# A hybrid attention and delta-rule layer on one core: a price for product changes in the planner, the last transposes in runs of eight, and a new slab order

## The chip, the cores and the metric

The kernel runs on one core of one Trainium2 chip. The metric is the device time of one execution in microseconds (us). Each time is the median of several executions of the same program.

## What is computed

One layer of a bidirectional encoder trunk: 512 tokens, 1024 channels, float32 throughout. In short:

```python
h = rms_norm(x, norm_pre)
aq, ak, av, az, dq, dk, dv, db, da, dz, gate_att, gate_dn = split_cols(h @ w_in)

q, k = rope(rms_norm(heads(aq))), rope(rms_norm(heads(ak)))       # 8 and 2 heads of 128
o_att = softmax(q @ k.T / sqrt(128)) @ v
y_att = (o_att * silu(az)) @ w_br_att

qkv = silu(short_conv(concat(dq, dk, dv), conv_w))                # 5 taps, 8 heads of 128
o_dn = bidir_gated_deltanet(l2(q), l2(k), v, decay(da), beta(db)) # chunks of 64, both directions
y_dn = (rms_norm(o_dn) * silu(dz)) @ w_br_dn

mix = (sigmoid(gate_att) * y_att + sigmoid(gate_dn) * y_dn) @ w_out
x1 = x + rms_norm(mix, norm_post)
out = x1 + rms_norm(sigmoid(x1 @ w_ple_gate) * (p @ w_ple_proj), ple_norm)
```

Inside the delta rule each chunk needs the inverse of a unit triangular matrix, and a scan over the chunks in each direction carries a state per head.

## The kernel before

**Two kinds of products.** The wide projections run as sums of three products of rounded parts: each operand is split into a high part and a low part, and low x high, high x low and high x high are added up. One step is three products with 512 columns; eight steps make one *slab* of 128 output channels (`gemm_t`, L542 to L559). These are called long products here. The delta rule, and the transposes by TensorE, use plain float32 products with 128 columns or fewer. These are the short ones.

**Two chains.** The delta rule is done for two groups of four heads, one after the other. `chain` starts `phase_a` (products of keys with keys and queries, then the substitution and the block steps of the inverse) and then two generators of `phase_b`, one for each direction; these are the scan. In a scan each product (L1202, L1213, L1222, L1240, L1254, four heads at once) waits for an operation of VectorE or ScalarE on the one before it. `phase_y` normalises the result of a group and transposes it.

**The planner.** The order of every instruction on each engine is made in Python when the kernel is built, by the class `Flow`. Parts of the kernel are generators, each with a priority (a smaller number goes first). They yield what they want: a time (`at`), an event (`ev`), a free buffer (`get`), or TensorE for so many us (`pe`). `Flow.run` (L124 to L157) keeps a clock, takes the ready part with the best priority, and moves the clock on by the time of TensorE that the part names, 0.682 us for a step of three long products, 0.9 us for four heads of short ones. Operations of the other engines are given a duration, find the first free place in a list of their engine's busy times (`fit`, `slot`, `op`), and are put into the program in that order of time. On the chip the order on each engine is what this gave; the times are what the hardware makes of them.

**The stream of slabs.** One generator, `stream`, with the last priority 10, goes through the list ORDER: `dq`, `dk`, `dv` (delta queries, keys and values by head), `dz`, `az`, `gA`, `gB` (gates), then the blocks `kv`, `q0`, `q1`, and behind the attention `ydn`, `yatt`, `out0`, `out1`, `pg0`, `pg1`. So TensorE does a step of a slab whenever no short product is ready. The weights are loaded from HBM in the same order (`fetch`, the queue of SyncE), and split in `loader`: the high part by ScalarE, the low part by VectorE or GpSimd (POOL). `split` (L254 to L266) chooses POOL if it ends sooner than VectorE plus a margin, COOL in general, HOT while `chains` is above 0, which is during the substitution and the probability products of the heads.

**Attention heads and what follows.** `att_heads` does four heads: sixteen score products, softmax without its division, then sixteen blocks of probabilities that are split on ScalarE and VectorE and multiplied with the values (L1734) in a ring of buffers in unit u14. Scores take a bank of PSUM of the kind `mm` while more than SPAREMM of them are free, and of the kind `aux` otherwise. The first two slabs of `yatt` are done together (`yatt_two`, L1838 on): their first half needs the first head group, their second half the second group. `vec` in the list starts the loads of the two vectors of the last norms (`vec_load`).

**The end.** `out0` and `out1` make the mix for four blocks of 128 rows. `out1_tail` adds the normalised mix to x, giving x1, and brings x1 into transposed form for the last products: row block 0 through VectorE and the DMA queues, blocks 1 to 3 by TensorE, for each half of 512 channels a scaling, four transposes (L1969) and a split. `pg0` and `pg1` are the gate products of the per-layer input.

**Other numbers.** SPARE lists windows of the planner's clock in which unused buffers are lent to the loader (`lend`). EXPS is a margin by which `prep` chooses between four exponentials on ScalarE (L983) and an addition on VectorE with one exponential (L987). EOUT is the earliest time on the planner's clock at which the product of p is stored; VGAP is the distance of the loads of values. PR holds priorities.

Of the kernel before, what the change touches and what calls it, by code (L numbers as in the profile page):

```python
# [35 lines left out]
class Flow:  # L36
# [7 lines left out]
    def __init__(self, slots):  # L44
        self.now = 0.0
        self.eng = {}
        self.slots = {k: [0.0] * n for k, n in slots.items()}
        self.parts = []
        self.later = []
        self.n = self.steps = 0  # L50
        self.shut, self.link = None, lambda a, b: None

# [66 lines left out]
    def flush(self):  # L119
        while self.later and self.later[0][0] <= self.now + 1e-9:  # L120
            _, _, fn, a, k = heapq.heappop(self.later)
            fn(*a, **k)  # L122

    def run(self):  # L124
        while self.parts:
            best, soon = None, None
            for p in self.parts:
                r = self.ready(p[3])
                if r is None:
                    continue  # L130
                if r <= self.now + 1e-9:
                    if best is None or p[:2] < best[:2]:
                        best = p
                elif soon is None or r < soon:
                    soon = r
            if best is None:
                if soon is None:
# [7 lines left out]
            try:  # L145
# [4 lines left out]
                continue  # L150
            if want[0] == "pe":
                self.now += want[1]
                self.steps += 1
                want = ("at", self.now)
# [5 lines left out]
ORDER = """  # L160
dq1 dk2 dk1 dk0 dq3 dk3 dq0 dq2 dv2 az4 dq6 az3 dk5 dv3 dq4 gB6
gA2 dk4 az7 dz1 dz4 dv1 gB5 dz2 az6 dv0 gB0 dq5 dq7 dk6 gB4 dk7
gA0 az0 gB3 dz6 dv6 dv7 gA6 gA5 dv4 dz0 az2 kv dv5 gB2 vec gA7
gB1 az1 dz3 az5 gA3 dz5 q0 dz7 gA1 q1 gA4 gB7 free_h ydn1 ydn2 ydn6
ydn3 ydn0 ydn5 ydn7 ydn4 yatt7 yatt4 yatt6 heads_on0 yatt3 yatt5 yatt0 yatt2 yatt1 heads_on1 out0
out1 pg0 pg1
"""
OUT0 = 'yatt3 yatt1 yatt2 yatt4'
PR = dict(dec=5, dm1=2, y=7, conv=1, gate=6, kv=4, q=9, head=7, ple=9, prep=1, tab=9)
GAP = 0.0  # L170
EXPS = 0.11
SP13 = 480.0
SPARE = ((15, "raw", 7.0, 190.0), (11, "pair", 22.0, 80.0), (12, "pair", 22.0, 80.0), (14, "pair", 279.0, 375.0),
         (13, "pair", 443.0, SP13), (6, "pair", 560.0, 640.0), (14, "raw", 590.0, 640.0))
EOUT = 27.01
WIDE = 2.0
LAND = "c2"
QTURN = (0,)
TURNED = 1
# [4 lines left out]
PVB = 0.695  # L184
VGAP = 1.5
HEADHOT = 1
BATCH, TURN = 4, 0.3
SPAREMM = 2
W1 = 0
COOL, HOT = 10.41, -0.29  # L190


@with_exitstack
def layer(ctx, tc, x, xT, pw0, wp1, wt, wba, wn, rows, qkn, hd16, npost, pnorm, dnorm, cs, out):
# [42 lines left out]
    def unit(i, shape, dt=F32):  # L237
        return tile(f"u{i}", shape, dt)
# [220 lines left out]
    slab, blocks, fetched = {}, {}, {}  # L459
    taken, weighed = Event(), Event()  # L460

# [3 lines left out]
    def lend(u, kind, t0, t1):  # L465

        yield "at", t0
        yield "get", f"u{u}"
        w = unit(u, [128, 2, 1024], F32 if kind == "raw" else F32R)
# [1162 lines left out]
    def att_heads(g):  # L1632
# [61 lines left out]
        yield "get", "u14"  # L1694
        ring = unit(14, [128, 2, 2, 16, 32], F32R)
        for i in range(2):
            F.slots[f"ring{i}"] = [F.now]
# [238 lines left out]
    def out1_tail(t, o, need):  # L1936
# [10 lines left out]
        for half, src in enumerate((late["mx0"][:, t, :], o)):  # L1947
# [5 lines left out]
            if t < TURNED:  # L1953
# [8 lines left out]
                ends.append((L, te))  # L1962
                continue
            yield "at", tr + 0.3
            yield "get", "aux"
            pt = bank("aux", [128, 4, 128])
            for j in range(4):
                k = half * 4 + j
                pe.transpose(pt[:, j, :], xa[:, k * 128:(k + 1) * 128], ident)  # L1969
            yield "pe", 0.436  # L1970
            cc = slice(t * 128, (t + 1) * 128)
            _, te = split(pt, x1Th[half][:, :, cc], x1Tl[half][:, :, cc], F.now, 512)
            free("aux", te)
        for half, (L, te) in enumerate(ends):
            yield "at", te - 0.5
            te = landed(L, te, x1Th[half], x1Tl[half], t)
        return te + 0.2
# [271 lines left out]
```

## Time and profile before

| | us |
|---|---|
| median of 3 runs | 733.78 |
| the three runs | 733.13, 733.86, 733.78 |
| the profiled execution | 732.72 |
| its span | 731.0 |

The profile holds one execution. PE is TensorE's products, PEld its weight loads, DVE is VectorE, ACT ScalarE, POOL GpSimd, SP SyncE. In rows of the timeline stand start, duration, engine, line, operation, output and input by the program's names, and in brackets the idle time ahead and what ended it. Products are pipelined: a product of 512 columns is shown with 0.39 us, while the next starts 0.23 us later. The kernel's two chains lie between 88 and 427 us, the heads between 490 and 600, the end of the list behind that. Most of VectorE's operations carry the line of a helper (L97 or L122), so they are told apart by their tiles: `whi` and `wlo` are a slab's high and low part, `wraw` what was loaded, `mm` and `aux` banks of PSUM, `u` a large unit of SBUF, `c`, `f`, `blk`, `go`, `gi` smaller buffers.

### The profile page before, as it was taken

The page shows a single profiled execution, that of the slowest core. Times are in us where ns is not written, and L with a number is a line of the kernel's source. Part 1 is how long each engine was busy: PE and PEld are TensorE (multiplying, and loading weights), DVE is VectorE, ACT ScalarE, POOL GpSimd, SP SyncE. Part 2 cuts the span into 40 slices and gives each one's busy share as a digit, 9 for nine tenths or more (in the row PEclk, how much of TensorE's full clock was granted, in tenths as well). Part 3 has the DMA queues.
Part 4 walks back from the last instruction along what each step waited for, and adds up shares of the span by engine and source line. Part 5 has one row for each costly group of instructions (what it writes and reads, how often), then busy time and mean ns, then how long its engine had stood idle before and what let it go on. Part 6 is the DMA issues. An engine that isn't in the chain of part 4 may idle for free.

```text
span 731.0 us, 12273 instructions
## 1 busy us (share of the span) xinstructions
PE 718.7 (98%) x4577; PEld 601.3 (82%) x4577; DVE 496.2 (68%) x914; ACT 352.6 (48%) x669; POOL 307.4 (42%) x293
## 2 busy tenths in 40 slices
PE   9999999999999999999999999999999999999996
PEld 7688888888789898888888888888888778888885
DVE  4688979889785667896946443658979974314534
ACT  6658653753651365435442236345746554323522
POOL 5836495111421265114411145655344638163501
PEclk9999999999999999999999999999999999999999
DMA  9854529856421324767350234695468568337313
GB/s 355 301 175 133 195 87 282 265 173 230 103 96 37 101 101 113 234 202 201 121 158 15 87 115 142 198 226 155 163 196 207 192 220 309 135 95 256 110 57 117
DMA packets 79051, 121.64 MB, mean 166 GB/s; under 512 B 24400, under 2 KB 42768, under 8 KB 78992
## 3 DMA queue, kind: packets, MB, share of 16 engines
q1 hardware_dynamic: 78848, 120.73, 52.4%
q8 instruction: 36, 0.59, 0.3%
q14 instruction: 23, 0.19, 0.1%
q10 hardware_dynamic: 144, 0.13, 0.1%
HBM read 94.98 MB, written 25.85 MB: 165 GB/s over the span
## 4 chain that ended last, share of the span: by engine, by line
PE 85%; DVE 8%; ACT 3%; issue 2%; DMA 1%; POOL 1%; POOLq 0%; SPq 0%; DVEq 0%; ACTq 0%
PE mm L553 15%; PE mm L555 14%; PE mm L554 14%; PE mm L574 4%; PE mm L572 4%; PE mm L573 4%; PE mm L592 3%; PE mm L590 3%; PE mm L591 3%; DVE f L122 3%; PE aux L1222 2%; PE aux L1254 2%; PE aux L1240 2%; PE aux L1213 1%; PE aux L1202 1%
## 5 line engine op out<-in xcount | busy, mean ns | idle before, releaser
L553 PE MATMUL mm<-u,wlo 128*128 128x512 f32 x488 | 195.9, 402 | 0.4 <-DVE wlo L97 0.4
L555 PE MATMUL mm<-u,whi 128*128 128x512 f32 x488 | 190.4, 390 | 0.0
L554 PE MATMUL mm<-u,whi 128*128 128x512 f32 x488 | 190.2, 390 | 0.0
L102 POOL TENSOR_TENSOR wlo<-wraw,whi 128x1024 fp32r<-128x1024 f32 x47 | 113.0, 2406 | 178.4 <-ACT whi L122 146.9
L553 PEld LDWEIGHTS mm<-u,wlo 128*128 128x128 f32 x488 | 91.8, 188 | 19.7 <-ACT u L122 0.8
L555 PEld LDWEIGHTS mm<-u,whi 128*128 128x128 f32 x488 | 91.6, 188 | 19.7
L554 PEld LDWEIGHTS mm<-u,whi 128*128 128x128 f32 x488 | 91.8, 188 | 17.0
L122 ACT CAST whi<-wraw 128x1024 fp32r<-128x1024 f32 x61 | 63.9, 1047 | 57.6 <-PE mm L555 20.1
L122 DVE SCALAR_TENSOR_TENSOR f<-mm,cw,f 128x510 f32<-128x510 f32 (+1 forms) x96 | 71.4, 746 | 9.0 <-ACT f L122 6.6
L102 POOL TENSOR_TENSOR u<-wraw,u 128x1024 fp32r<-128x1024 f32 x18 | 43.1, 2403 | 27.6 <-ACT u L122 26.0
L572 PE MATMUL mm<-u,u 128*128 128x512 f32 (+1 forms) x136 | 51.8, 381 | 0.0
L574 PE MATMUL mm<-u,u 128*128 128x512 f32 (+1 forms) x136 | 51.3, 377 | 0.0
L573 PE MATMUL mm<-u,u 128*128 128x512 f32 (+1 forms) x136 | 51.2, 377 | 0.0
L122 DVE TENSOR_TENSOR u<-aux,u 128x512 f32<-128x512 f32 (+2 forms) x49 | 31.6, 664 | 12.9 <-PE aux L1043 6.4
L122 ACT COPY c<-aux 128x512 f32<-128x512 f32 x18 | 10.4, 585 | 48.2 <-DVE f L122 35.4
L590 PE MATMUL mm<-whi,u 128*128 128x512 f32 x80 | 31.4, 393 | 0.0
L122 ACT ACTIVATE mm<-f 128x512 f32<-128x512 f32 x24 | 14.4, 600 | 35.0 <-DVE f L122 35.0
L592 PE MATMUL mm<-whi,u 128*128 128x512 f32 x80 | 31.2, 390 | 0.0
L591 PE MATMUL mm<-wlo,u 128*128 128x512 f32 x80 | 31.1, 389 | 0.0
L102 POOL TENSOR_TENSOR u<-u,u 128x1024 fp32r<-128x1024 f32 (+1 forms) x11 | 22.0, 2004 | 20.9 <-ACT u L122 15.6
L574 PEld LDWEIGHTS mm<-u,u 128*128 128x128 f32 x136 | 25.6, 188 | 4.8
L573 PEld LDWEIGHTS mm<-u,u 128*128 128x128 f32 x136 | 25.6, 188 | 4.6
(297 smaller groups left out, 1504.2 us busy)
## 6 DMA issues: line engine op xcount, KB each, us to landing
wraw<-in_wt_dram SPq DMA_DIRECT2D x58, 512.0 KB, 3.6
wraw<-in_wn_dram SPq DMA_DIRECT2D x24, 512.0 KB, 4.1
u<-in_wt_dram SPq DMA_DIRECT2D x14, 512.0 KB, 6.3
u<-CI SPq DMA_DIRECT2D x16, 256.0 KB, 5.5
u<-VD SPq DMA_DIRECT2D x16, 256.0 KB, 6.7
u<-in_x_dram SPq DMA_DIRECT2D x4, 512.0 KB, 7.6
u<-in_xT_dram SPq DMA_DIRECT2D x4, 512.0 KB, 8.2
eD<-u SPq DMA_DIRECT2D x8, 256.0 KB, 9.0
```

Source lines behind the costliest of these rows:

```text
L102: ins = fn(*a, **k)
L122: fn(*a, **k)
L553: pe.matmul(o, lo[:, k, :], mh(k), start=(k == 0), stop=False)
L554: pe.matmul(o, hi[:, k, :], ml(k), start=False, stop=False)
L555: pe.matmul(o, hi[:, k, :], mh(k), start=False, stop=(k == 7))
L572: pe.matmul(o, b, hi, start=(i == 0), stop=False)
L573: pe.matmul(o, a, lo, start=False, stop=False)
L574: pe.matmul(o, a, hi, start=False, stop=(i == 7))
L590: pe.matmul(o[t], b, hi, start=(k == 0), stop=False)
L591: pe.matmul(o[t], a, lo, start=False, stop=False)
L592: pe.matmul(o[t], a, hi, start=False, stop=(k == 7))
L1222: pe.matmul(pw[:, h, :], Vm[g][d][:, 4 * c + h, :], r[:, h, :], start=True, stop=True)
```

## The change

Three things are changed.

1. `Flow.run` knows which generators make short products in float32 (`is_exact`). Whenever TensorE goes from one of them to any other part, the planner's clock is moved on by SWAP = 0.09 us. A new method, `later_than`, can hold such a part back for up to DEFER us, if another one will be ready by then, and let the stream go first. DEFER is 0.0.
2. In `out1_tail`, for row blocks 1 to 3, the two halves are scaled first, then eight transposes stand in one run over two banks, then the two splits.
3. ORDER, OUT0 (the places of out0's loads among the slabs), priorities and margins are other ones. In ORDER `vec` moves from the middle to a place behind the last `yatt`. One lending of u14 (from 590 us of the planner's clock) now waits until the second head group has taken its ring there.

```diff
+    def is_exact(p):
+        return p[2].__name__ in ("phase_a", "phase_b", "phase_y", "q_tail", "kv_tail", "out1_tail")
+
+    def later_than(self, p):
+
+        since = self.put.setdefault(p[1], self.now)
+        if self.now >= since + DEFER or not any(
+                q is not p and self.is_exact(q) and q[3][0] == "at" and self.now < q[3][1] <= since + DEFER for q in self.parts):
+            self.put.clear()
+            return None
+        ways = [q for q in self.parts if not self.is_exact(q) and q[2].__name__ == "stream" and q[3][0] == "at"
+                and q[3][1] <= self.now + 1e-9]
+        return ways[0] if ways else None
...
+            if best is not None and not self.exact and self.is_exact(best):
+                best = self.later_than(best) or best
...
             if want[0] == "pe":
+                exact = self.is_exact(best)
+                if self.exact and not exact:
+                    self.now += SWAP
+                self.exact = exact
                 self.now += want[1]
...
-dq1 dk2 dk1 dk0 dq3 dk3 dq0 dq2 dv2 az4 dq6 az3 dk5 dv3 dq4 gB6
-gA2 dk4 az7 dz1 dz4 dv1 gB5 dz2 az6 dv0 gB0 dq5 dq7 dk6 gB4 dk7
-gA0 az0 gB3 dz6 dv6 dv7 gA6 gA5 dv4 dz0 az2 kv dv5 gB2 vec gA7
-gB1 az1 dz3 az5 gA3 dz5 q0 dz7 gA1 q1 gA4 gB7 free_h ydn1 ydn2 ydn6
-ydn3 ydn0 ydn5 ydn7 ydn4 yatt7 yatt4 yatt6 heads_on0 yatt3 yatt5 yatt0 yatt2 yatt1 heads_on1 out0
+dq2 dk3 dk2 dk0 dq3 dk1 dq0 dq1 dv2 az2 dk6 dv3 dq7 dq6 dk5 gA2
+dz5 az0 dv1 dz7 dz4 gB0 az5 dz2 gA3 az3 dv0 gB2 dk7 dq4 dq5 gB1
+dk4 dz1 gA4 az1 dv6 dv4 gB7 gB4 dz0 dv7 kv dv5 az4 gB5 gA1 gA7
+gB6 gB3 gA0 dz3 q0 az7 az6 dz6 q1 gA6 gA5 free_h ydn4 ydn1 ydn5 ydn6
+ydn2 ydn0 ydn3 ydn7 yatt2 heads_on0 yatt0 yatt6 yatt3 yatt5 yatt4 yatt1 yatt7 vec heads_on1 out0
 out1 pg0 pg1
-OUT0 = 'yatt3 yatt1 yatt2 yatt4'
-PR = dict(dec=5, dm1=2, y=7, conv=1, gate=6, kv=4, q=9, head=7, ple=9, prep=1, tab=9)
+OUT0 = 'yatt3 yatt7 yatt6 yatt0'
+PR = dict(dec=1, dm1=2, y=9, conv=1, gate=6, kv=5, q=0, head=5, ple=1, prep=3, tab=3)
-EXPS = 0.11
+EXPS = -0.24
-EOUT = 27.01
+EOUT = 25.2
+SWAP, DEFER = 0.09, 0.0
-VGAP = 1.5
+VGAP = 1.2
-SPAREMM = 2
+SPAREMM = 1
-COOL, HOT = 10.41, -0.29
+COOL, HOT = 9.89, -1.3
...
+        if u == 14 and t0 > 500.0:
+            yield "ev", ringed
...
-            yield "at", tr + 0.3
+        for half, (L, te) in enumerate(ends):
+            yield "at", te - 0.5
+            te = landed(L, te, x1Th[half], x1Tl[half], t)
+        if t < TURNED:
+            return te + 0.2
+        yield "at", tr + 0.3
+        pts = []
+        for half in range(2):
             yield "get", "aux"
-            pt = bank("aux", [128, 4, 128])
+            pts.append(bank("aux", [128, 4, 128]))
+        for half, pt in enumerate(pts):
             for j in range(4):
                 k = half * 4 + j
                 pe.transpose(pt[:, j, :], xa[:, k * 128:(k + 1) * 128], ident)
-            yield "pe", 0.436
+        yield "pe", 0.872
```

More of the change, by code (lines that the diff above doesn't have):

```diff
@@ L50, in __init__ @@
         self.n = self.steps = 0
+        self.exact, self.put = False, {}
         self.shut, self.link = None, lambda a, b: None
@@ L122, in flush @@
             fn(*a, **k)
+    @staticmethod
+    def is_exact(p):
[9 more added lines that the diff above has]
+        return ways[0] if ways else None
     def run(self):
@@ L459, in layer @@
     slab, blocks, fetched = {}, {}, {}
-    taken, weighed = Event(), Event()
+    taken, weighed, ringed = Event(), Event(), Event()
     lent = {"raw": {}, "pair": {}}
@@ L1695, in att_heads @@
         ring = unit(14, [128, 2, 2, 16, 32], F32R)
+        if g == 1:
+            ringed.set(F.now)
         for i in range(2):
@@ L1962, in out1_tail @@
                 ends.append((L, te))
-                continue
-            yield "at", tr + 0.3
+        for half, (L, te) in enumerate(ends):
[6 more added lines that the diff above has]
+        for half in range(2):
             yield "get", "aux"
-            pt = bank("aux", [128, 4, 128])
+            pts.append(bank("aux", [128, 4, 128]))
+        for half, pt in enumerate(pts):
             for j in range(4):
@@ L1969, in out1_tail @@
                 pe.transpose(pt[:, j, :], xa[:, k * 128:(k + 1) * 128], ident)
-            yield "pe", 0.436
-            cc = slice(t * 128, (t + 1) * 128)
+        yield "pe", 0.872
+        cc = slice(t * 128, (t + 1) * 128)
+        for half, pt in enumerate(pts):
             _, te = split(pt, x1Th[half][:, :, cc], x1Tl[half][:, :, cc], F.now, 512)
             free("aux", te)
-        for half, (L, te) in enumerate(ends):
-            yield "at", te - 0.5
-            te = landed(L, te, x1Th[half], x1Tl[half], t)
         return te + 0.2
```

## The prediction

> **What bounds the kernel now.** I read the head of the page first, then the waits of TensorE (PE), then the stages, then PE's rows in order of time.
>
> ```profile
> span 731.0 us, 12273 instructions
> PE 718.7 (98%) x4577; PEld 601.3 (82%) x4577; DVE 496.2 (68%) x914; ACT 352.6 (48%) x669; POOL 307.4 (42%) x293
> PE 85%; DVE 8%; ACT 3%; issue 2%; DMA 1%; POOL 1%; POOLq 0%; SPq 0%; DVEq 0%; ACTq 0%
> ```
>
> PE is busy for 98% of the span, and 85% of the chain that ends last is PE. The change adds and removes no product, so nearly all of the 718.7 us stays. What an order can win is in the other 731.0 - 718.7 = 12.3 us. The waits of PE, longest first, say where some of it lies:
>
> ```profile
> PE mm L2110 <- POOL ident masks.py:199: 1.4, 1, 1.4
> PE mm L1861 <- DVE u L97: 0.7, 1, 0.7
> PE aux L1132 <- issue: 0.7, 1, 0.7
> PE mm L1861 <- POOL wlo L102: 0.6, 1, 0.6
> ...
> PE mm L881 <- DVE partk L122: 0.3, 1, 0.3
> ...
> PE aux L1486 <- DVE f L97: 0.3, 1, 0.3
> ```
>
> The 1.4 us ahead of the warm-up stay. The others shown are 0.7 + 0.7 + 0.6 + 0.3 + 0.3 = 2.6 us. Two of the three longest are in L1861, the first product group of the attention branch's output, which stands around the second head group's probability products.
>
> ```profile
> 90.00:190.00 100.00, 100.00 (x471) 83.62 (x471) 86.70 (x156) 55.52 (x121) 38.92 (x35) 1.00 0.68 204
> 210.00:265.00 55.00, 54.94 (x392) 49.42 (x391) 34.45 (x91) 21.52 (x41) 17.82 (x14) 1.00 0.22 72
> 530.00:600.00 70.00, 68.65 (x581) 55.42 (x582) 58.11 (x88) 40.06 (x73) 32.28 (x33) 1.00 0.63 194
> 600.00:725.00 125.00, 123.93 (x581) 103.41 (x579) 48.98 (x73) 43.52 (x77) 54.83 (x44) 1.00 0.47 164
> 725.00:731.00 6.00, 0.00 (x0) 0.00 (x0) 1.83 (x5) 0.81 (x3) 1.53 (x3) 0.82 0.26 87
> ```
>
> The columns are the stretch, its length, and busy time of PE, PEld, DVE, ACT and POOL, then the granted clock. In the substitution (90 to 190) PE has no gap, with DVE at 86.7%. In the first chain (210 to 265) PE lacks 0.06 us. The head stage (530 to 600) lacks 1.35 us, the largest loss in the middle. Behind 725 PE has ended and the last row is stored. The clock is 1.00 wherever PE works, so nothing is to be had there.
>
> A busy PE hides short waits, since the end of a product is modelled. Adding up start-to-start distances beyond the usual ones, I get waits of some 6 to 7 us behind the start, all told; this is my estimate, and the cap of any gain.
>
> **The price of a change.** The planner now adds 0.09 us to its clock whenever a long product follows a short one. What does such a change cost?
>
> ```profile
> 671.18 0.39 PE L573 MATMUL mm<-u,u 128*128 128x512 f32 x1
> 671.41 0.39 PE L574 MATMUL mm<-u,u 128*128 128x512 f32 x1
> 671.64 0.60 PE L1969 MATMUL aux<-ident,whi 128*128 128x128 f32 x4
> 671.99 0.48 PE L572 MATMUL mm<-u,u 128*128 128x512 f32 x1
> 672.31 0.40 PE L573 MATMUL mm<-u,u 128*128 128x512 f32 x1
> ...
> 238.69 0.39 PE L555 MATMUL mm<-u,whi 128*128 128x512 f32 x1
> 238.92 1.05 PE L1254 MATMUL aux<-c,u 128*128 128x128 f32 x8
> 239.73 0.48 PE L553 MATMUL mm<-u,wlo 128*128 128x512 f32 x1
> 240.05 0.39 PE L554 MATMUL mm<-u,whi 128*128 128x512 f32 x1
> ```
>
> The first long product behind a run (671.99, 239.73) shows 0.48 us for 0.39, and 0.32 to the next start for 0.23: that looks like a price of 0.09. But it also starts early. From the last long product before the run to the second behind it: 672.31 - 671.41 = 0.90 with four short ones, 240.05 - 238.69 = 1.36 with eight. Two long ones take 2 x 0.23 = 0.46 of each. So four short ones and a change take 0.44, eight and a change 0.90; the difference gives 0.115 for a short one, and 0.44 - 0.46 = -0.02 for the change. Within the 0.01 of the rows' rounding, **a change costs 0 to 0.01 us**, not 0.09.
>
> The Trainium skill ("TensorE: Matmul & The Clock Gate", section "LDWEIGHTS (loading the stationary operand)") puts a weight load at its columns over 1.2 GHz, 107 ns for 128. If that load of the first long product stood bare behind a run, three changes fewer at the end would give 3 x 0.107 = 0.32 us (an estimate from that page). The rows above show no such cost, and the sum goes by them.
>
> **The change part by part.**
>
> *Price.* No instruction is added. The code yields at most 62 short groups in each chain (8 of keys and queries, 16 of the inverse, 34 in the two scans, 4 of the transposes behind) and 14 in the tails of kv, q and x1: 138 x 0.09 = 12.4 us at most by which the planner's clock runs slower; it does not set instructions' durations, only their order. In each gap of a scan that is filled with steps of three long products (0.68 us), 0.09 is 13% of a step; so some 13% of the gaps may get one step fewer. 68 scan groups x 0.13 = 9 gaps. Each costs between 0 (the operand was ready) and 0.68 us: 0 to 6 us. I take 0.05 a gap, +0.45 us, because the first chain's 55 us today lack only 0.06, that is, operands are mostly ready when PE comes.
>
> *Holding back.* DEFER is 0.0, so the test in later_than is true on its first call, and it always returns None. Nothing is held. 0 us.
>
> *x1 in runs of eight.* Rows 1 to 3 do both halves' scaling first, then eight transposes, then the splits. Three changes fewer: 0 to 0.03 us. The first half is ready later by one scaling and half a run, about 1.2 us; who waits?
>
> ```profile
> 690.90 0.69 DVE L122 TENSOR_TENSOR u<-aux,u 128x512 fp32r<-128x512 f32 x1 [1.20 <-ACT u L122]
> ...
> 696.48 0.39 PE L573 MATMUL mm<-u,u 128*128 128x512 f32 x1
> ```
>
> The last split of row 3 ends at 691.6; its gate product starts near 696.5. The cover is 4.9 us, and a second bank of aux is free there. 0 us.
>
> *Norm vectors later.* Their two loads are moved behind the last yatt slab.
>
> ```profile
> 595.00 0.64 SPq L122 DMA_DIRECT2D blk<-in_npost_dram  x1
> 596.58 0.33 SPq L122 DMA_DIRECT2D blk<-in_pnorm_dram  x1
> ...
> 639.19 0.69 DVE L122 TENSOR_TENSOR u<-mm,blk 128x512 f32<-128x512 f32 x1 [2.65 <-PE mm L574]
> ```
>
> The first reader runs at 639.19, after the first out0 group, which takes 24 x 0.23 = 5.4 us. A load behind yatt is issued near 634 at the earliest and lands within these 5 us or up to some 3 us late; then DVE waits with one of five mm banks held, and PE goes on with the next. 0, at the outside +0.5 us; and SP is freed of two issues (0.97 us) while gates and slabs are wanted at 595.
>
> *Splits on DVE or POOL, and the order.* HOT goes from -0.29 to -1.3: while a chain or the probability products run, a slab's low part goes to POOL only where that ends 1.3 us sooner.
>
> ```profile
> L102 POOL TENSOR_TENSOR wlo<-wraw,whi 128x1024 fp32r<-128x1024 f32 x47 | 113.0, 2406 | 178.4 <-ACT whi L122 146.9
> ...
> L97 DVE TENSOR_TENSOR wlo<-wraw,whi 128x1024 fp32r<-128x1024 f32 x14 | 17.2, 1227 | 2.1 <-ACT whi L122 2.0
> ...
> 574.54 2.85 POOL L102 TENSOR_TENSOR wlo<-wraw,whi 128x1024 fp32r<-128x1024 f32 x1
> ...
> 574.31 4.23 DVE L97 TENSOR_TENSOR blk<-u,blk 128x512 fp32r<-128x512 f32 x3 [0.38 <-ACT blk L122]
> 578.47 0.68 DVE L97 TENSOR_TENSOR c<-u,c 128x512 fp32r<-128x512 f32 x1
> ...
> 576.46 0.39 PE L555 MATMUL mm<-u,whi 128*128 128x512 f32 x1
> 577.45 0.50 PE L1861 MATMUL mm<-u,wlo 128*128 128x512 f32 x1 [0.60 <-POOL wlo L102]
> ...
> 592.32 2.11 PE L1861 MATMUL mm<-u,u 128*128 128x512 f32 x8 [0.69 <-DVE u L97]
> ```
>
> A split costs 2.41 us on POOL, 1.23 on DVE. At 574.54 one meets the splits of the probabilities: three DVE operations take 4.23 us for about 3 x 0.68 = 2.04, and PE starts at 577.45, 0.99 behind 576.46 for a usual 0.23. That is 0.76 us lost. At 592.32 PE waits 0.69 for a slab split queued behind those operations. A new slab order and the new thresholds place both anew. Bounds: -0.76 - 0.69 = -1.45 if both go, 0 if the like returns, +2.2 (the DVE time that this collision cost) if a second is made. I take -1.3, nearest to the first row: such a meeting is an accident of a slab's turn. For the waits at L881 and L1486 (0.3 + 0.3), and the rest of the estimate of 6 to 7 us (small gaps in scans), I take -0.75 of a possible -3.
>
> *The rest.* The first ten slabs keep their kinds (q, k, k, k, q, k, q, q, v, az), so the start is the same. EXPS only makes ACT's four-fold exponentials rarer; VGAP starts each next row of values 0.3 us sooner; EOUT moves eight stores 1.8 us in the planner; SPAREMM lets a score take a bank when two are free; the other priorities decide ties. PE has no gap where these run, and I find no bound beyond the same gaps: 0, with +-1 us in the range.
>
> Sum: +0.45 - 1.3 - 0.75 = **-1.6 us**. The profiled execution took 732.72 us (731.0 and 1.72 around it), 1.06 below the median of 733.78. So 732.72 - 1.6 = 731.1 by the profiled execution, **732.2 us** as a median.
>
> **The rivals.**
>
> *A, the forecast:* the head stage's two waits go, little else: 731.0 to 732.9. Chance 0.45, two thirds of it under 732.3 (0.30 faster, 0.15 same).
>
> *B, waits change places:* the new order has as many accidents as the old; the price gains nothing, since a change costs nothing. 733.8 +- 1. For it: 2.6 us of listed waits are few already. Chance 0.22, all same.
>
> *C, the price starves the scans:* the planner believes PE busier than it is, so it fills each gap behind a run with less. From about 0.35 us of wait in each of the 9 gaps it outweighs A: 9 x 0.35 = 3.1, less the 1.3 of the head stage = +1.8, 735.6; with the full 0.68, 738.6. Against it: operands come early today. For it: PE is 100% busy, so a filler that is not planned is a hole. Chance 0.23 (0.22 slower, 0.01 same).
>
> *D, the order also clears the chains:* half of the cap of 6 to 7 us and more, 3.5 to 4.5: 729.3 to 730.3. Chance 0.10, faster.
>
> Faster by over 0.2% (1.5 us, about what a measurement of this kernel can tell from no change): 0.40; within: 0.38; slower: 0.22. The range leaves out the far half of D and the worst third of C: 729.8 to 736.5. A's own range is 731.0 to 732.9.
>
> **What would show it.** Right: PE's busy time within 1 us of 718.7; a first long product behind a run still shows 0.48, and the distance across it no price; L1861's waits under 0.5 us together; x1 with eight transposes in a row and the same gap-free 600 to 725. Wrong: waits of PE in the scans, at the scan lines L1202 to L1254, of over 2 us together (C), or new waits on POOL or DVE splits in the head stage that replace the old (B); a wait of out0 on the norm vectors would show my cover of 5 us wrong. It all falls if PE's own busy time moves by several us.

## The result, and the profile after

The changed kernel takes 738.42 us (median of 738.31, 740.57 and 738.42) where the kernel before takes 733.78. The ratio is 1.0065, with a 95% interval of 1.0048 to 1.0082: slower, by about 4.6 us. The forecast was 732.2, with a range up to 736.5. The rows below read from the profiled execution of the changed kernel; its lines stand 25 to 32 further down than before (L553 is L578, L1202 L1227, L1861 L1888), and the helpers L97 and L122 are L98 and L123. A plain float32 product of the code stands as two rows in the trace (four heads are `x8`), a transpose by TensorE or a long product as one; "products" counts rows below.

The head of the page first: span, busy time by engine, and the shares of the chain that ends last.

```profile
span 736.0 us, 12292 instructions
...
PE 720.2 (98%) x4577; PEld 601.8 (82%) x4577; DVE 499.4 (68%) x918; ACT 348.9 (47%) x645; POOL 303.9 (41%) x292
...
PE 72%; DVE 13%; ACT 7%; issue 3%; POOL 3%; DMA 1%; POOLq 0%; SPq 0%; ACTq 0%; DVEq 0%
```

PE does the same 4577 products, so the 5.0 us of span are not added work, though it counts as busy for 1.5 us longer. What changed is the chain: PE's share falls from 85 to 72%, and DVE's rises from 8 to 13, ACT's from 3 to 7. The shares tell which engine the chain runs through, not how long PE stood: 13% of the span are 96 us. The waits of PE (engine, line, what it waited for; total us, times, longest):

```profile
PE mm L578 <- DVE wlo L98: 2.1, 2, 1.7
PE aux L1157 <- issue: 2.0, 2, 1.3
PE mm L2142 <- POOL ident masks.py:199: 1.4, 1, 1.4
PE mm L578 <- POOL wlo L103: 0.8, 1, 0.8
PE aux L1227 <- ACT c L123: 0.6, 1, 0.6
...
PE aux L1227 <- ACT blk L123: 0.2, 1, 0.2
PE aux L1265 <- DVE f L123: 0.2, 1, 0.2
```

L1861, two of the three longest before, is gone from the list. In its place stand a slab's low part on DVE (L578), a wait that only "issue" explains (L1157), another low part on POOL, and the scans' lines L1227 and L1265. The stages, with the columns of the table shown before:

```profile
95.00:195.00 100.00, 98.30 (x454) 81.77 (x453) 84.34 (x151) 49.00 (x89) 37.47 (x34) 1.00 0.63 199
213.00:271.00 58.00, 57.00 (x434) 49.80 (x430) 36.66 (x93) 23.47 (x45) 18.48 (x15) 1.00 0.18 60
535.00:603.00 68.00, 67.95 (x581) 55.56 (x581) 58.00 (x90) 42.44 (x76) 27.78 (x31) 1.00 0.64 187
603.00:728.00 125.00, 125.00 (x585) 104.58 (x584) 48.63 (x70) 41.45 (x72) 56.26 (x44) 1.00 0.48 164
```

The substitution (95 to 195) lacks 1.70 us, which it did not before; the first chain lacks 1.00 for 0.06; the heads lack 0.05 for 1.35; behind them there is no gap.

Busy time hides short waits, because the end of a product is modelled. So I also added up, for each product, the distance from its start to the next start beyond the usual one (0.227 us for 512 columns, 0.112 for 128). This is my own sum over the trace's rows, and it accounts for the span's difference:

| PE's waits, us | before | after |
|---|---|---|
| to the first chain's block steps | 5.66 | 7.69 |
| block steps of the first chain | 1.71 | 1.78 |
| **first scan** and its edges | 1.34 | 4.08 |
| to the second chain's block steps | 0.17 | 0.19 |
| block steps of the second chain | 1.38 | 2.22 |
| second scan and its edges | 1.28 | 1.55 |
| to the first probability products | 0.26 | 1.35 |
| **heads**, to the last probability products and the slab behind | 3.62 | 1.67 |
| the rest | 0.00 | -0.15 |
| sum | 15.42 | 20.38 |

The difference is 4.96 us, for 736.0 - 731.0 = 5.0 of span. The heads give 1.95 us back, a little more than was forecast. The first scan alone takes 2.74 more. The rest of the loss is in three places: 2.03 ahead of the first block steps, 1.09 ahead of the probabilities, 0.84 in the second block steps. One execution's sum for the long first row differs by about 1.6 us between kernels that are alike there (5.33, 6.96 and 5.97 in e8, e10 and e13 below), so only what a single row shows is read there. The first scan's sum is steady: between its first and last product it is 3.8 to 4.0 us in the changed kernel, e3, e8 and e10, which have the same order there, and 1.0 to 1.1 in the kernel before, e4 and e9.

### The profile page after: what moved, and what is told of

Same layout as the page of the kernel before. It is cut to its first block, busy times and chain, and to the rows that moved or that the text cites. A ratio compares the mean times of both kernels' runs of the same rounds, so it can differ in the third digit from the quotient of the medians.

```text
span 736.0 us, 12292 instructions
## 1 busy us (share of the span) xinstructions
PE 720.2 (98%) x4577; PEld 601.8 (82%) x4577; DVE 499.4 (68%) x918; ACT 348.9 (47%) x645; POOL 303.9 (41%) x292
## 4 chain that ended last, share of the span: by engine, by line
PE 72%; DVE 13%; ACT 7%; issue 3%; POOL 3%; DMA 1%; POOLq 0%; SPq 0%; ACTq 0%; DVEq 0%
PE mm L578 11%; PE mm L580 11%; PE mm L579 11%; DVE f L123 7%; PE mm L597 4%; PE mm L598 4%; PE mm L599 4%; PE mm L615 3%; PE mm L617 3%; PE mm L616 3%; DVE u L123 3%; PE aux L1761 2%; PE aux L1279 2%; PE aux L1247 2%; PE aux L1227 2%
## 5 line engine op out<-in xcount | busy, mean ns | idle before, releaser
L578 PE MATMUL mm<-u,wlo 128*128 128x512 f32 x488 | 195.8, 401 | 2.9 <-DVE wlo L98 2.1
L103 POOL TENSOR_TENSOR wlo<-wraw,whi 128x1024 fp32r<-128x1024 f32 x46 | 110.3, 2401 | 157.3 <-ACT whi L123 143.7
L578 PEld LDWEIGHTS mm<-u,wlo 128*128 128x128 f32 x488 | 91.7, 188 | 22.6 <-DVE wlo L98 2.1
L123 ACT CAST whi<-wraw 128x1024 fp32r<-128x1024 f32 x60 | 62.9, 1049 | 56.4 <-PE mm L580 22.8
L123 DVE SCALAR_TENSOR_TENSOR f<-mm,cw,f 128x510 f32<-128x510 f32 (+1 forms) x96 | 71.4, 746 | 9.0 <-ACT f L123 6.6
L123 DVE TENSOR_TENSOR u<-aux,u 128x512 f32<-128x512 f32 (+2 forms) x49 | 31.6, 665 | 9.6 <-ACT u L123 4.4
L123 ACT ACTIVATE mm<-f 128x512 f32<-128x512 f32 x24 | 14.4, 601 | 37.8 <-DVE f L123 37.8
L103 POOL TENSOR_SCALAR_AFFINE_SELECT u<-u 128x512 f32<-128x512 f32 x16 | 10.1, 638 | 53.4 <-DVE wlo L98 23.6
L123 ACT COPY c<-aux 128x512 f32<-128x512 f32 x18 | 10.5, 588 | 41.7 <-DVE f L123 22.0
```

The lines of the kernel that those rows point to most:

```text
L103: ins = fn(*a, **k)
L578: pe.matmul(o, lo[:, k, :], mh(k), start=(k == 0), stop=False)
```

## The experiments

Two theories stood at the outset. **Price**: the planner charges 0.09 us for something that costs nothing on the chip, fills the scans too thinly, and PE waits there. **Order**: any new order has its accidents (a split on the wrong engine, a late operand), and these are merely other ones. Times are medians, ratios are against the kernel before in the same session, and "waits in the scan" are the sums of the last section between a scan's first and last product: before 1.04 in the first and 1.22 in the second, after 3.81 and 1.49.

### The parts of the change, one at a time

**e1**: the kernel before, with the price alone. (Its edit brings the code of point 1 of the change and the rule on the lending of u14 along; in this order the plan is the same with that rule and without it. So it is in e5, e6, e7 and e11.)

```diff
...
+SWAP, DEFER = 0.09, 0.0
...
```

> The kernel before with its own order and settings and only the price of 0.09 us. Theory P (the price leaves the scans without filler): 736 to 738, with at least four more waits of 0.2 to 0.4 us at the scan lines than the kernel before has. Theory O (the new order and settings put loads and splits in each other's way; the price is harmless): 733 to 735, scan waits as before. Theory K (the time follows where the planner's own clock ends, without what the price adds to it: 734.1 - 70 x 0.09 = 727.8 against 726.0 for the kernel before): 735.6.

744.72 us, ratio 1.0146 (1.0121 to 1.0170). The price alone costs an untouched order more than the whole change does, and more than any of the three theories allowed. The first scan's waits are 3.65 us, which is what the price theory had in mind; the time is not.

**e2**: the changed kernel with `SWAP = 0.0`.

> The kernel after with the price set to 0 and everything else kept. Theory P: 733 to 736. Theory O: 737 to 740, the wait of a slab behind the start of the substitution still there. Theory K: the planner's clock ends at 748.7 here, which would be some 755: the order is made for the price and falls apart without it.

763.19 us, ratio 1.0395 (1.0379 to 1.0410), outside all three ranges; nearest is theory K, by which the order falls apart without the price. The first scan's waits fall to 1.71, but the second scan now stands without slabs to fill it. The order of the changed kernel only fits the planner that it was made with. So neither e1 nor e2 gives "the price's share" of the time: each is a plan disturbed. What the planner itself believes makes this plain. Its clock when the list ends, and what that is made of (from the planner when the kernel is built, not from the chip):

```
                      end of plan   idle in it   price in it   span on chip
before                   725.96       11.20         0              731.0
before, price .09        734.13       13.07        70 x 0.09       743.4
after                    729.23        8.92        65 x 0.09       736.0
after, price 0           748.70       34.2          0              761.4
```

Under the priced clock the new order is 4.9 us better than the old (729.23 against 734.13). Against the old order under the old clock, it is 3.27 worse on paper. It holds 5.85 us of price that the chip doesn't charge, so without the price the same plan would be 2.6 us better than before; the chip made it 5.0 worse. So some 7.6 us of waits came that the planner didn't see. They can't simply be put down to the price: without any, the new order takes 761.4 - 748.70 = 12.7 us more than its plan, and with it 736.0 - (729.23 - 5.85) = 12.6. The old order takes 5.0 us more than its plan without the price, and 743.4 - (734.13 - 6.30) = 15.6 with it. Each line is a plan of its own, so this is a hint and not a proof.

**e3** and **e4**: the changed kernel with the old four-by-four transposes of x1, and the kernel before with x1 in runs of eight.

```diff
...
-        yield "pe", 0.872
...
+            yield "pe", 0.436
...
```

> The kernel after with the transposes of x1 in runs of four as before. All theories: within 1 us of the kernel after (738.4), since a change of product costs nothing and the stretch from 600 us on has no gap; over 1 us either way would mean that the runs of eight matter.

> The kernel before with only the runs of eight for x1 (no price). All theories: within 1 us of 733.8. If it is slower by over 1 us, the planner's places for other work shift with any edit, and a single number says little about the edit itself.

e3: 737.46 us, 1.0047 (1.0032 to 1.0062). e4: 734.29 us, 1.0004 (0.9995 to 1.0014). No effect of the runs of eight can be seen: e4's interval leaves -0.4 to +1.0 us, and e3's overlaps that of the changed kernel.

### How much price, and where

**e5, e6, e7, e11, e12** each change one number or one name: SWAP 0.045 or 0.18 in the kernel before; the price charged everywhere but in the scans (before, then after), or in the scans only.

```diff
-        return p[2].__name__ in ("phase_a", "phase_b", "phase_y", "q_tail", "kv_tail", "out1_tail")
+        return p[2].__name__ in ("phase_b",)
```

> The kernel before with a price of 0.045. Looked at for the first scan alone (the stretch of the scan products of the first head group), where the waits of TensorE beyond the usual start-to-start distances are 1.0 us without a price and 3.7 to 4.0 with 0.09. Theory P (each priced change hands its time back as a wait): 2.0 to 2.9 us. Theory O (waits follow the arrangement, not the price): anything, as likely under 1.5 or over 3.7.

> The kernel before with a price of 0.18; first scan again. Theory P: 5 to 7.5 us of waits. Theory O: no relation, 1 to 4 us.

> The kernel before with the price of 0.09, except for changes out of a scan (phase_b). Theory P: the first scan is back at 1.0 to 1.5 us of waits, while the total stays above 736 since the rest of the order is still disturbed. Theory O: the first scan has 3 to 4 us as with the full price.

> The kernel before with the price of 0.09 us charged only behind the scans' own products (phase_b). The plan charges 1.35 us within the first scan and 1.71 within the second. Theory (what the plan charges in a scan, the chip spends there waiting, since the chip charges nothing): waits of PE beyond usual distances of 2.3 to 3.4 us in the first scan (1.04 before) and 2.0 to 3.0 in the second (1.22 before). Rival (any disturbed order makes such waits, with a price or without): 1.0 to 1.7 in both, or waits unrelated to the charge. The whole time is not what this run is for: the order was tuned to another clock, and the plan itself idles 20.9 us for 11.2 before; some 744 us.

> The changed kernel with the price charged everywhere but behind the scans' products. In the first scan the plan charges 0 us (1.53 in the changed kernel) and puts 40 steps of other parts there for 32. Theory: the waits in the first scan fall from 3.81 to 1.0 - 2.4 us. Rival (the waits come with the changed kernel's order and priorities): 3.4 to 4.3 as in every run with its order and its price. The second scan is not to be read, since the plan runs out of slabs there and idles 15.3 us; the whole time some 760 us.

Each was run once, since the whole time (742.2, 756.96, 742.81, 742.33 and 765.0 us) mostly tells how badly a disturbed plan fits. The waits in the first scan beside what the plan charges in it, with the bare groups (short groups that wait and have no long step ahead of them) split off:

| | charged in the first scan | its waits | of these, bare groups | second scan: charged, waits |
|---|---|---|---|---|
| before | 0 | 1.04 | 0 | 0, 1.22 |
| e5, half price | 0.67 | 1.97 | 0 | 0.77, 1.89 |
| e1, price | 1.53 | 3.65 | 0.95 | 1.71, 2.07 |
| after | 1.53 | 3.81 | 1.10 | 1.26, 1.49 |
| e6, double price | 3.24 | 5.45 | 0.86 | 3.24, 3.30 |
| e2, after, no price | 0 | 1.71 | 0 | (no slabs left) |
| e7, not in scans | 0 | 2.46 | 0.73 | 0.27, 1.00 |
| e11, only in scans | 1.35 | **1.28** | 0 | 1.71, 2.49 |
| e12, after, not in scans | 0 | **3.27** | 1.10 | (no slabs left) |

Read down the first five rows, the waits rise with the price, and so they do in the second scan. But e11 charges 1.35 us in the first scan and has hardly a wait more; e7 and e12 charge nothing there and wait 2.46 and 3.27. The price theory misses three of the rows clearly (its expectations for e7, for e11's first scan and for e12 were not met) and e5's by 0.03 us. The order theory leaves the rise in the first five unexplained, and its ranges for e7 (3 to 4 us) and e12 (from 3.4) were missed as well. The charge inside a scan is neither needed nor enough. A reading that fits all rows is that a charge anywhere moves PE's place in the plan against the operands, and that this decides which groups find a filler; no run shows it directly.

Nor do the waits go with the amount of filler. Between the first and the last product of the first scan stand 84 long products before, 90 in the changed kernel, and 93 in e1: more steps, where the waits rose by 2.77 and 2.61 us. In the second scan the changed kernel has 63 for 84, seven steps fewer, and its waits rose by only 0.27.

### One bare group, made and unmade

The trace of the changed kernel at such a place. Columns: start, duration, engine, line, operation, tiles, and in brackets the idle time ahead.

```profile
226.90 1.05 PE L1247 MATMUL aux<-c,u 128*128 128x128 f32 x8
...
227.79 1.06 PE L1279 MATMUL aux<-c,u 128*128 128x128 f32 x8
227.99 0.69 DVE L123 TENSOR_TENSOR f<-aux,dj 128x512 f32<-128x512 f32 x1 [1.30 <-PE aux L1247]
228.76 0.59 ACT L123 COPY c<-aux 128x512 f32<-128x512 f32 x1 [3.53 <-issue]
...
229.40 1.16 PE L1227 MATMUL aux<-blk,u 128*128 128x128 f32 x8 [0.55 <-ACT c L123]
...
230.40 1.06 PE L1265 MATMUL aux<-f,u 128*128 128x128 f32 x8
```

And the like in the kernel before:

```profile
221.99 1.06 PE L1254 MATMUL aux<-c,u 128*128 128x128 f32 x8
222.19 0.69 DVE L122 TENSOR_TENSOR f<-aux,dj 128x512 f32<-128x512 f32 x1 [1.22 <-PE aux L1222]
...
222.80 0.48 PE L553 MATMUL mm<-u,wlo 128*128 128x512 f32 x1
...
222.97 0.59 ACT L122 COPY c<-aux 128x512 f32<-128x512 f32 x1 [1.74 <-DVE f L122]
...
223.61 1.16 PE L1240 MATMUL aux<-f,u 128*128 128x128 f32 x8
```

The products at L1247 fill a bank that DVE and then ACT read: the ACT copy starts 0.08 us behind the end of the DVE operation (227.99 + 0.69 = 228.68, 228.76), and 0.09 in the kernel before. The planner gives both the same start, since it makes each wait for PE only. So it takes the bank to be free some 0.7 us too early. L1227 doesn't read c, so what it waits for must be the bank. Before, a long step stands between (222.80), and covers just that. After, the plan found a bank free at once, put no step there, and PE stands from 228.69 (eight products of 0.112 behind 227.79) to 229.40. The Trainium skill ("PSUM — Partial Sum Buffer", section "PSUM bank collisions raise a hardware error") says that two engines may not touch one bank at once, reads included, and that the compiler adds a dependency between them. The trace agrees: the copy waits for its neighbour.

The same is behind three more of the changed kernel's seven waits of 0.15 us or more in its first scan. The second reader of a bank starts at 239.25, 250.29 and 261.22, 0.03 to 0.09 us behind the end of the first, and the short group that waits for it starts 0.24 us late each time, although two long steps stand ahead of it. The kernel before has one such wait there, 0.23 us behind the copy at 230.74. With the 0.71 of L1227 these make 1.43 of the seven's 2.13 us. The other bare group, 0.39 us late at 224.31, waits for an ACT copy of its own operand. No run has a planner that starts the second reader later, so what that alone would be worth is not shown.

**e14** takes that step away from there in the kernel before and puts it behind the next two short groups, and nothing else; **e13** gives the changed kernel one, on top of e8 (below), from three places further on. In both, one call of the stream is made at another turn of the planner's loop, and the planner's clock is not touched.

```diff
...
+            if best[2].__name__ == "stream" and self.late and self.now >= self.late[0] - 0.01:
+                self.late.pop(0)
+                want = ("pe", 0.682)
+            else:
+                want = next(best[2])
...
```

> The kernel before with the like taken away: the step of three long products that stands at 222.80 in its first scan, ahead of the state products (L1240) at 223.61, is moved behind the next two short groups, where a filler stands already. Theory: the state products now wait there for the ACT copy that ended at 223.56, 0.55 - 0.73 us and 0.10 for the restart, and what follows has more cover than it needs: the first scan's waits rise from 1.04 to 1.6 - 1.9 us, the whole time by 0.6 to 0.8 us (ratio 1.001). Rival: the group finds its operand ready (the copy only happened to end there), 1.0 - 1.2 us. If the chain of operands is what bounds the scan there, the wait is made good behind: 1.0 - 1.2 as well.

> The kernel of e8 with one step of three long products moved on PE by three places: from between the second step of its slab and the products behind it (planned at 228.41) to ahead of the keys-by-state products of the first scan planned at 225.40, which stood bare behind another short group and waited for an ACT copy (0.71 us beyond the usual distance, L1227). Theory now (a short group with no long step ahead of it shows that the plan took an operand or a bank for ready some 0.7 us too early; a filler hides it): that wait goes, and with it the 0.10 of its restart; nothing takes its place, and the first scan's waits fall from 3.98 to 3.1 - 3.4 us. Rival (the chain of operands bounds the scan there, so that the same time is waited one group later): 3.8 - 4.1 us. On the whole time 0.7 us at most: 736.2 - 737.4.

The kernel of e14, where the step was:

```profile
222.87 1.06 PE L1263 MATMUL aux<-c,u 128*128 128x128 f32 x8
223.07 0.69 DVE L123 TENSOR_TENSOR f<-aux,dj 128x512 f32<-128x512 f32 x1 [1.22 <-PE aux L1231]
223.85 0.59 ACT L123 COPY c<-aux 128x512 f32<-128x512 f32 x1 [0.96 <-DVE f L123]
...
224.49 1.16 PE L1249 MATMUL aux<-f,u 128*128 128x128 f32 x8 [0.56 <-ACT c L123]
```

The wait of the changed kernel is here, made in the kernel before by moving three products: PE idles 0.56 us, and 0.73 lie beyond the usual distance. The first scan's waits rise from 1.04 to 1.70, within the 1.6 to 1.9 expected, and the time is 735.14, ratio 1.0011 (1.0001 to 1.0021). The time behind did not make it good.

The kernel of e13, where the step was put:

```profile
226.88 0.48 PE L592 MATMUL mm<-u,wlo 128*128 128x512 f32 x1
...
227.67 1.16 PE L1241 MATMUL aux<-blk,u 128*128 128x128 f32 x8
...
229.83 1.12 DVE L1285 SCALAR_TENSOR_TENSOR blk<-blk,ex,aux 128x128 f32<-128x128 f32 x4 [2.88 <-PE aux L1279]
...
231.01 1.16 PE L1293 MATMUL aux<-c,u 128*128 128x128 f32 x8 [0.20 <-DVE blk L1285]
```

PE's idle time ahead of L1241 is gone. But the step was taken from in front of L1293, which now starts 0.37 us late, and the scan's waits fall from 3.98 only to 3.66, not to the 3.1 to 3.4 expected. So half of the wait came back one place further on, and both the theory's range and the rival's (3.8 to 4.1) were missed: around there one step more would be needed, not only another place for one. The time, 736.37 us, ratio 1.0031 (1.0019 to 1.0042), can't be told from that of e8.

### The accidents of the order

**e8**: the changed kernel with the low part of slab dv 1 on POOL instead of DVE. One instruction moves.

```diff
...
-        fn = (pool if eng == "POOL" else dve).tensor_sub
+        fn = (pool if eng == "POOL" or aside else dve).tensor_sub
...
```

> The kernel after with one instruction moved: the low part of the slab dv1 (the VectorE operation at 134.03 us, 1.19 us) is done by GpSimd at the same place of the plan. Theory S (TensorE's wait of 1.7 us at 133 to 135 comes from this operation standing in VectorE's queue behind the first step of the substitution, which waits for a transfer): the wait goes, 736.2 to 737.0. Rival: another wait takes its place, the next slab's low part or the first scan, 738.0 to 738.8.

What it is about, in the changed kernel:

```profile
132.19 0.69 DVE L98 TENSOR_SCALAR blk<-blk 128x1024 f32<-128x1024 f32 x1 [2.98 <-DMA blk<-dB]
...
134.03 1.19 DVE L98 TENSOR_TENSOR wlo<-u,whi 128x1024 fp32r<-128x1024 f32 x1
...
135.27 0.50 PE L578 MATMUL mm<-u,wlo 128*128 128x512 f32 x1 [1.70 <-DVE wlo L98]
135.29 0.65 POOL L103 TENSOR_SCALAR_AFFINE_SELECT u<-u 128x512 f32<-128x512 f32 x1 [7.60 <-DVE wlo L98]
```

DVE stood still for 2.98 us, because the first operation of the substitution awaited a DMA, and the split of a slab was queued behind that operation on the same engine. It came at 134.03, and PE stood for 1.70 us, while POOL had been idle for 7.60. In e8 the split runs on POOL, long before:

```profile
129.16 2.38 POOL L98 TENSOR_TENSOR wlo<-u,whi 128x1024 fp32r<-128x1024 f32 x1 [1.80 <-ACT whi L123]
```

The wait is gone, and the waits in that stretch fall from 7.69 to 5.33. The time is 737.12 us, a little above the 736.2 to 737.0 expected, ratio 1.0047 (1.0033 to 1.0060): lower than the 1.0065 of the changed kernel by about as much as this wait, but the intervals overlap, so the time by itself doesn't show it.

**e9** tests the forecast's own head-stage term on the kernel before: the low part of slab yatt 7 goes from POOL to DVE. **e10** does the same with ydn 5 in the kernel of e8.

```diff
...
+        fn = (pool if eng == "POOL" and not aside else dve).tensor_sub
...
-            _, tl = split(raw, hi, lo, t, 1024, True, soon=name is names[0])
+            _, tl = split(raw, hi, lo, t, 1024, True, soon=name is names[0], aside=name == ("yatt", 7))
```

> The kernel before, with the low part of one slab (yatt 7) formed on DVE instead of POOL; every instruction keeps its place in the plan. The forecast's head-stage term said that this split on POOL (2.85 us, beside three DVE operations that took 4.23 us for a usual 2.04) costs PE 0.76 us at 577.45. If that is the price, the span falls from 731.0 to 730.2 - 730.6 and the median by about 0.4 to 0.8 us, a ratio of 0.999. Rival: DVE is as full as POOL there and the 1.2 us of the split on DVE push the probability splits behind it, so the wait only changes its releaser: within 0.2 us of before. If DVE has no room at all: up to 1.2 us slower.

> The changed kernel with the low part of slab dv 1 on POOL, as in e8, and that of slab ydn 5 on DVE, whose end on POOL PE awaits at 527.9 in the changed kernel (0.97 us beyond the usual distance). Theory: both waits are accidents of where a slab's split lands, worth 1.9 and 0.97 us. Expected: no wait of over 0.3 us at ydn 5, span 733.0 - 733.4 (e8: 734.0), median 736.1 - 736.6. Even then it stays above before by some 2.5 us, which is the first scan's share (+2.7). Rival: DVE, which serves the softmax there, makes the next head products late by the 1.2 us: span 734.0 or more.

e9 takes 732.84 us, ratio 0.9978 (0.9968 to 0.9989): faster than both kernels. Its rows:

```profile
574.93 1.83 DVE L102 TENSOR_TENSOR wlo<-wraw,whi 128x1024 fp32r<-128x1024 f32 x1
...
576.68 1.88 DVE L97 TENSOR_TENSOR blk<-u,blk 128x512 fp32r<-128x512 f32 x3
...
577.53 0.39 PE L555 MATMUL mm<-u,whi 128*128 128x512 f32 x1
...
577.75 0.39 PE L1861 MATMUL mm<-u,wlo 128*128 128x512 f32 x1
```

The three splits of probabilities take 1.88 us for 4.23, the slab's split 1.83 for 2.85, and L1861 starts 0.22 us behind the product ahead: the 0.76 us are gone. The heads' waits fall from 3.62 to 2.62. The profiled execution's span is no shorter (731.1), since its waits ahead of both chains' block steps and in the first chain's are longer by 1.1 us together; the gain is read from the medians, which give 1.6 us (0.8 to 2.3). That is more than the 0.4 to 0.8 expected, and more than these rows account for. The Trainium skill ("SBUF — State Buffer", section "SBUF: two separate sides") has DVE and POOL share a pair of ports of which one engine has exclusive use for a whole instruction, among other cases if DVE's operation has two inputs in SBUF and POOL's reads SBUF, as here. The trace agrees: of the three operations, which lost 4.23 - 1.88 = 2.35 us, a single one took 2.89 us for a usual 0.68. It started at 575.06, while POOL's split ran, and ended 0.56 us behind that split's end at 577.39. POOL's split, which started at 574.54 while DVE's first operation ran, took 2.85 us for a mean of 2.41.

e10 is a miss: 737.98 us, ratio 1.0047 (1.0031 to 1.0062). The row that waited for POOL at 527.89 in the changed kernel now waits as long for DVE:

```profile
526.60 0.50 PE L578 MATMUL mm<-u,wlo 128*128 128x512 f32 x1 [0.81 <-DVE wlo L103]
```

The split took 1.95 us on DVE, and one of the probability splits came 0.7 us late for L1761, so that the heads' waits rise by a further 0.97. The rival held: DVE has no room there either.

## Why the prediction was wrong

**Two terms of the sum failed: the price, and the other waits.** The price term was put at +0.45 us: nine gaps with one step fewer, at 0.05 us each, "because the first chain's 55 us today lack only 0.06, that is, operands are mostly ready when PE comes". Measured, the two scans lost 2.77 + 0.27 = 3.0 us between their first and last products, 0.34 for each of the nine gaps. The bounds (0 to 6 us) held it; the choice within them did not. It was wrong for two reasons, and whether the price made these waits at all is open.

- *The 0.06 was read from busy time*, and the prediction itself says that busy time hides short waits. By start-to-start distances the same scan had 1.04 us of waits. (The estimate of 6 to 7 us for all waits behind the start was low too: the table has 15.42 - 5.66 = 9.76 from the first block steps on.) And e14 shows that what its products need, there a bank, is not free early: one step taken away is one wait of 0.73 us.
- *Thinner filling was the wrong picture.* The sum counts all 68 scan groups as gaps, but only (1.53 + 1.26) / 0.09 = 31 of them are charged a price, so by its own rule 4 gaps lose a step. And no step was lost where the waits came: the first scan has 90 long products for 84. What the rows show instead is single places. Two groups go ahead bare, 0.39 and 0.71 us late, and others are 0.15 to 0.24 late behind their filler. The 0.71 and three of the 0.24 come from the second reader of a bank, which the planner has end some 0.7 us early (rows of the changed kernel; e14 makes one such wait).

This is near rival C, priced at 0.35 us for each gap to give 735.6, and at 738.6 with the full step; it was given 0.23. The place (the scans) and the size (3.0 for 3.1 us) are as it had them, but its mechanism, less filler in each gap, is not what the rows show. That the time lies near its 738.6 is luck, since other waits than those of the scans make up the rest. How the loss divides between price and order can't be settled by these runs: without the price the new order falls apart (e2), the price alone spoils the old one (e1), and in e11 and e12 the charge and the waits go apart.

**The other waits** were put at -0.75 and came out at +4.05 (2.03 + 0.07 + 0.02 + 0.84 + 1.09 by the table, of which the 2.03 is uncertain by 1.6). This is the larger miss of the two, 4.8 us against 2.6. The sum took from these waits only what could be won, and for what the new order might add it put 0, with 1 us either way in the range. New ones: dv 1 at the start of the substitution (1.70 idle), ydn 5 on POOL (0.81), and the stops among the block steps below (+0.84 in the second chain's). That is rival B's mechanism, accidents of the order, but they did not merely change places: two of the three came where PE had next to none before (the substitution, and 0.26 us ahead of the probabilities). PE's busy time moved by 1.5 us, too, where at most 1 was expected.

**Right, by the profile:**

- *A change of products costs nothing that the rows can show.* In the changed kernel it is so as well:

```profile
675.16 0.39 PE L599 MATMUL mm<-u,u 128*128 128x512 f32 x1
...
675.39 1.04 PE L2003 MATMUL aux<-ident,whi 128*128 128x128 f32 x8
...
676.19 0.48 PE L597 MATMUL mm<-u,u 128*128 128x512 f32 x1
...
676.50 0.39 PE L598 MATMUL mm<-u,u 128*128 128x512 f32 x1
```

  From 675.16 to 676.50 are 1.34 us; two long products take 0.454 and eight short ones 8 x 0.112 = 0.896, which leaves -0.01. The Trainium skill's load time of 107 ns ("TensorE: Matmul & The Clock Gate", section "LDWEIGHTS (loading the stationary operand)") doesn't stand bare at a change. In the trace a load is shown with 0.19 us (187 to 188 ns at L1888), beside the product ahead. e4's interval of 0.9995 to 1.0014 is too wide to tell a gain of 0.3 us from none.
- *x1 in runs of eight*, 0 us: the rows show the run of eight, and 603 to 728 has no gap.
- *The head stage*, put at -1.3 us, gave -1.95. Both waits of L1861 are gone; the view of its new line L1888 has an empty list of waits:

```profile
L1888 PE MATMUL mm<-u,u x16: 389/389/389, 595.2 to 602.2; 128*128 128x512 f32 x16
...
its engine sat idle before it (us, times) until:
who waited for it (us, times):
```

  e9 shows that the 0.76 us were read rightly: the wait goes with the split. The reason by HOT was wrong, though: with HOT put back to -0.29 the planner gives the very same order (its plan, not a run), so it was the slabs' turn that moved the splits.
- *Norm vectors*, 0 us. They are issued where they were expected, near 634, and no wait for them is in the list:

```profile
633.22 0.43 SPq L123 DMA_DIRECT2D blk<-in_npost_dram  x1
...
633.75 0.37 SPq L123 DMA_DIRECT2D blk<-in_pnorm_dram  x1
```

- *Holding back*, 0 us: DEFER is 0.0 in every kernel here; no run has another value.

So the forecast got the gain that it named, and lost it three and a half times over (4.96 + 1.95 = 6.9 us) in waits that it did not see coming: 3.0 us in the scans and 4.05 elsewhere, less 0.15 in the rest.

## What to carry to other kernels

Before a planner is given a new cost, measure the cost on the chip as a distance across the event, not as the duration of the row behind it: 0.48 for 0.39 us looked like a price, and the distance showed none. An order is then arranged for the clock that it is given: here the new one is 4.9 us better on a clock by which the old one had lost 8.2. In a kernel whose engine is full, read slack from start-to-start distances, not from busy time, and ask of every gap what happens with one filler fewer: where the planner's model is early, the filler may be hiding it, as e14 shows for one place.

## What was not expected of the hardware

*A start behind a wait costs a little more than the wait.* Eight short products that wait for an operand take 0.99 to 1.00 us to the next start (229.40 to 230.40 in the changed kernel) where they take 0.89 behind another product (226.90 to 227.79). It is the first of the eight, 0.21 us for 0.11 to the next start, in 19 of the 20 groups of the scans of both kernels that start over 0.03 us late. So each wait in a scan costs 0.10 us beside its idle time.

*PE stops in step with the fetching of instructions.* In the block steps 128 rows of PE, for 64 products of 32 x 32, follow each other closely, and the changed kernel stops among them:

```profile
360.74 1.24 PE L1157 MATMUL aux<-u,c 32*32 32x32 f32 x123
...
363.26 0.25 PE L1157 MATMUL aux<-u,c 32*32 32x32 f32 x5 [1.29 <-issue]
```

No operand is awaited that the profile shows; the stop starts where a 16 KB packet of the instruction queue ends, which took 1.75 us there, for a median of 1.15 over this queue's 36 such packets. In the 16 traces of this case there are 24 such stops of over 0.1 us, and 23 of them begin 1.6 to 2.2 us behind the start of such a packet. The longer the packet, the longer the stop: 0.4 to 0.9 us between two starts with packets of up to 1.2 us, 1.1 to 1.5 with packets of 1.5 to 1.8. So the cause is likely, but no run was made to show it. Kernels with the same order and the same products lost between 0.9 and 2.0 us of idle time by it (e10 and the changed kernel), so part of the 0.84 above belongs to the execution and not to the order.
